# One decoder layer on one core: stick-breaking weights kept as plain products, the last value of each group added at the end, and both instruction plans made anew

## The chip, the cores and the metric

The kernel runs on one core of a Trainium2 chip. The metric is the device time of one execution in microseconds, the median of the runs. Times of single instructions come from one profiled execution.

## The reference, cut to what matters

One layer on x of 1024 tokens by 1024 channels in float32: RMSNorm, one input projection, attention and a convolution module side by side, one output projection with a residual, RMSNorm, a gated up-projection with a short convolution, and a down-projection with a residual. The part that the change touches:

```python
beta[t, s] = sigmoid(q[t] . k[s] / 8)                     # s < t, 8 heads of 64
A[t, s]    = beta[t, s] * prod over s<j<t of (1 - beta[t, j])
o[t]       = sum over s<t of A[t, s] * v[s]
...
x = x + concat([attention, conv]) @ w_out
```

With P[t, s] = the product over s <= j < t of (1 - beta[t, j]), A[t, s] = P[t, s+1] - P[t, s]. So the sum can be written with differences of neighbouring values of v in place of differences of P.

## The kernel before, in words

TensorE takes each float32 product in three passes (high by high, low by high, high by low; `mm3`, L389 to L391), so most operands are made twice: a rounded high copy (mostly on ACT) and a low remainder (VectorE or POOL). Five stages follow each other in the span.

- **Input projections (0 to about 220 us).** Two loads of x per step are squared (L530), scaled (L548), turned (`hT` L556) and split (`h_hi` L560, `h_lo` L561). Weights of v come as `raw_v`, and are scaled into `hi_v` (L593) and `lo_v` (L599); glu weights go through L606 to L622, qk after them. `begin` (L485 to L499) runs idle matmuls while x loads.
- **Attention (about 220 to 411 us).** Heads go one after another, in halves, and queries in groups of 256. For each 128 queries: scores `z` (L1304, L1305) on TensorE, sigmoid(-z) into `nb` on ACT (L1312), a reversed scan of products on VectorE (L1326), `less`, which takes one from the result, on POOL (L1331) or ACT (L1333), transposes `wT` on TensorE (L1353), the high copy (`rest`, or `diagonal` for the block on the diagonal; L1362, L1364), the low (`tl` L1374, `diagonal` L1369), and products `po` with v's differences (L1381). Beyond a query P is one; less one, it is zero there, so keys up to the group's end add nothing. `differences` forms v[s-1] - v[s] once, through `ahead`, which SyncE's DMAs fill with v a row later. Of each `po`, ACT copies one half of the head pair's rows (L1409) and VectorE adds the other half to it (L1412, 64x512) into `attn`. Between these TensorE runs the qk projection and the conv rows of w_out (`op`); the weights of w_out come as `rawo`, with highs `w_hh` and `hio` and lows `w_hl` (L1439) and `loo` (L1531).
- **Handover (about 411 to 492 us).** For each token tile in the order 0, 4, 1, 5, 2, 6, 3, 7: the attention rows of w_out (`opa`; its operand `m` is cast on ACT, L1599 and L1607, with its low on VectorE, L1605 and L1608), the addition to x (L1622), the square on ACT (L1632), the root on POOL, the scaling to `h2` (L1640), the transposes `h2T` (L1648) and the operands `b` and `bT` of a seven-product block scheme (L1660, L1661, sums `raws` and `t`, L1673 to L1698). The first blocks of w_up are `rawu0` and `rawu1`, their operands `a` and `aS` (L385, L386, L1784, L1788). x is stored by tile to `x_d` (L1626).
- **Up-projection (492 to 886 us)** and **down-projection (886 to 1095 us)**, `u`, `u_S` and `dn`.

The work up to the attention's end is one plan and the handover another. Each is a list of operations with a cost and due time; `in_order` issues them on TensorE, VectorE, ACT and POOL in the order of a table of numbers, `ORDERS`, of 1929 and 237 entries, so an instruction runs behind all that stand ahead of it on its engine. An operation that may run on several engines goes by the plan's costs to the one that is free first. SyncE issues the DMAs in one queue, in which one that waits holds those behind it.

## Time and profile before

| | us |
|---|---|
| median of 3 runs | 1103.04 (1102.15 to 1103.22) |
| profiled execution | 1100.73 |
| its span | 1099.0 |
| TensorE busy | 1085.8 |
| VectorE busy | 875.4 |
| ACT busy | 606.6 |
| POOL busy | 609.8 |
| `less` on POOL, 57 instructions | 39.8 |

The profiled execution is 1.7 us longer than its span (work ahead of the first and behind the last recorded instruction). In the profile PE is TensorE, PEld its weight loads, DVE VectorE, POOL GpSimd, and SP SyncE. A row gives the start in us, the duration, the engine, the line, the operation, output <- inputs, shapes and count; a bracket at its end is the engine's idle time just before, with the instruction that ended it.

### The profile page before, as it was taken

Reading aid. Unit: us, or ns where it says so; the run is one execution under the profiler, and the core shown is the slowest. Engines: PE = TensorE matmul, PEld = TensorE weight load, DVE = VectorE, ACT = ScalarE, POOL = GpSimd, SP = SyncE. Lnnn points to the kernel's source line nnn. Section 1 sums busy time; section 2 is a strip of 40 time slices with the busy share of each in tenths; the row PEclk is TensorE's granted clock in tenths of the full one; section 3 lists DMA queues with packets and bytes.
Section 4 is the critical chain, followed back from the end, with each engine's and each line's share of the span. In section 5 each row is a group of like instructions: output and inputs, shape, how many; then the busy total and the mean of one; then the engine's idle time right before and its main releaser. Section 6 shows DMA issues by size and latency. Waiting matters only on the chain.

```text
span 1099.0 us, 14945 instructions
## 1 busy us (share of the span) xinstructions
PE 1085.8 (99%) x5252; PEld 904.1 (82%) x5252; DVE 875.4 (80%) x1178; ACT 606.6 (55%) x1113; POOL 609.8 (55%) x540
## 2 busy tenths in 40 slices
PE   8999999999999999999999999999999999999998
PEld 5888888889888878778888888888888888888887
DVE  6498898689998996899977777677867578697885
ACT  7345467878877665644433333333433388676660
POOL 3377988786654544784333223313322399887760
PEclk9999999999999999999999999999999999999999
DMA  8121210444643324523322312222222572413403
GB/s 272 39 58 52 83 39 19 116 154 143 203 125 97 106 94 161 187 58 116 96 96 67 104 59 96 77 96 77 77 97 67 183 287 78 153 31 124 153 7 147
DMA packets 110249, 117.99 MB, mean 107 GB/s; under 512 B 21114, under 2 KB 89953, under 8 KB 110175
## 3 DMA queue, kind: packets, MB, share of 16 engines
q1 hardware_dynamic: 110158, 117.05, 32.5%
q8 instruction: 41, 0.67, 0.3%
q14 instruction: 34, 0.27, 0.1%
q10 hardware_dynamic: 16, 0.00, 0.0%
HBM read 82.43 MB, written 28.31 MB: 101 GB/s over the span
## 4 chain that ended last, share of the span: by engine, by line
PE 92%; DVE 3%; ACT 1%; DMA 1%; issue 1%; POOL 1%; SPq 0%; DVEq 0%; ACTq 0%
PE dn L1987 19%; PE u_S L391 7%; PE u_S L390 7%; PE u_S L389 7%; PE u L391 5%; PE u L390 5%; PE u L389 5%; PE po L1381 3%; PE qk L389 3%; PE qk L391 3%; PE qk L390 3%; PE wT L1353 2%; PE z L1304 1%; PE glu_b L390 1%; PE op L389 1%; PE glu_b L391 1%
## 5 line engine op out<-in xcount | busy, mean ns | idle before, releaser
L1987 PE MATMUL dn<-wd,wd 128*128 128x512 f32 x768 | 181.4, 389 | 0.0
L1987 PEld LDWEIGHTS dn<-wd,wd 128*128 128x128 f32 x768 | 144.1, 188 | 29.9
L1990 DVE TENSOR_TENSOR c<-dn,c 128x512 f32<-128x512 f32 x120 | 81.4, 685 | 27.6 <-PE dn L1987 27.0
L391 PE MATMUL u_S<-bT,aS 128*128 128x512 f32 x264 | 102.7, 389 | 0.1
L390 PE MATMUL u_S<-bT,aS 128*128 128x512 f32 x264 | 102.5, 389 | 0.0
L389 PE MATMUL u_S<-bT,aS 128*128 128x512 f32 x264 | 102.5, 389 | 0.0
L385 ACT CAST aS<-rawu 128x512 fp32r<-128x512 f32 x63 | 39.0, 621 | 95.2 <-PE u_S L391 68.9
L1892 ACT CAST wd<-rawd 128x512 fp32r<-128x512 f32 x128 | 72.6, 618 | 31.8 <-DMA rawd<-act_d 8.0
L1326 DVE TENSOR_TENSOR_SCAN nb<-nb,one 128x128 f32<-128x128 f32 (+7 forms) x64 | 85.1, 1341 | 1.5 <-ACT nb L1312 1.4
L1733 POOL TENSOR_TENSOR s<-rawu 128x512 f32<-128x512 f32 x21 | 29.6, 1414 | 101.8 <-DMA rawu<-in_w_up_dram 101.8
L1891 ACT COPY whole<-rawd 128x512 f32<-128x512 f32 x110 | 63.4, 585 | 26.0 <-DVE wd L1893 12.9
L1739 POOL TENSOR_TENSOR rawu<-rawu 128x512 f32<-128x512 f32 x21 | 29.5, 1408 | 81.1 <-DVE a L386 81.1
L1893 DVE TENSOR_TENSOR wd<-whole,wd 128x512 fp32r<-128x512 f32 x90 | 59.9, 684 | 12.6 <-ACT wd L1892 6.8
L1331 POOL TENSOR_SCALAR nb<-nb 128x512 f32<-128x512 f32 (+7 forms) x57 | 39.8, 705 | 50.3 <-DVE nb L1326 38.0
L1836 DVE SCALAR_TENSOR_TENSOR y<-gv,cols_a,y 128x1023 f32<-128x1023 f32 (+1 forms) x44 | 59.9, 1361 | 8.9 <-ACT y L1834 8.9
L385 ACT CAST a<-rawu 128x512 fp32r<-128x512 f32 x63 | 38.9, 621 | 48.7 <-PE u_S L391 33.8
L389 PE MATMUL u<-b,a 128*128 128x512 f32 x168 | 65.5, 390 | 0.0
L391 PE MATMUL u<-b,a 128*128 128x512 f32 x168 | 65.4, 389 | 0.0
L390 PE MATMUL u<-b,a 128*128 128x512 f32 x168 | 65.3, 389 | 0.0
L386 DVE TENSOR_TENSOR a<-rawu,a 128x512 fp32r<-128x512 f32 x63 | 50.9, 809 | 13.3 <-ACT a L385 13.3
L1735 POOL TENSOR_TENSOR rawu<-s,rawu 128x512 f32<-128x512 f32 x21 | 32.0, 1527 | 48.6 <-DVE a L386 47.8
L391 PEld LDWEIGHTS u_S<-bT,aS 128*128 128x128 f32 x264 | 49.5, 188 | 10.7 <-DVE aS L386 0.5
(359 smaller groups left out, 3274.5 us busy)
## 6 DMA issues: line engine op xcount, KB each, us to landing
rawu<-in_w_up_dram SPq DMA_DIRECT2D x44, 512.0 KB
act_d<-y SPq DMA_DIRECT2D x22, 512.0 KB
rawd<-act_d SPq DMA_DIRECT2D x22, 512.0 KB
rawd<-in_w_down_dram SPq DMA_DIRECT2D x22, 512.0 KB
raw_qk<-in_w_in_dram SPq DMA_DIRECT2D x16, 256.0 KB
rawo<-in_w_out_dram SPq DMA_DIRECT2D x8, 512.0 KB
m<-conv_d SPq DMA_DIRECT2D x16, 256.0 KB
xt<-in_x_dram SPq DMA_DIRECT2D x8, 512.0 KB
```

The costliest lines, as they stand in the source:

```text
L385: nc.scalar.copy(hi, src)
L386: lo_engine.tensor_tensor(lo, src, f32(hi), op=ALU.subtract)
L389: nc.tensor.matmul(ps, a_hi, b_hi, start=first, stop=False)
L390: nc.tensor.matmul(ps, a_hi, b_lo, start=False, stop=False)
L391: nc.tensor.matmul(ps, a_lo, b_hi, start=False, stop=last)
L1326: nc.vector.tensor_tensor_scan(rev, rev, ones_of[0][:, :w], 0.0, op0=ALU.mult, op1=ALU.max)
L1836: nc.vector.scalar_tensor_tensor(y[:, j:], g[:, :S - j], par("fw", (KF - 1 - j) * NF + f), y[:, j:], op0=ALU.mult, op1=ALU.add)
L1891: nc.scalar.copy(whole, src)
L1892: nc.scalar.copy(t[:, 0], src)
L1893: lo_engine.tensor_tensor(t[:, 1], whole, f32(t[:, 0]), op=ALU.subtract)
L1987: nc.tensor.matmul(ps, a[:, tok], b, start=first and m == 0, stop=last and m == 2, skip_group_check=True)
L1990: nc.vector.tensor_tensor(sums[c][s], ps, sums[c][s], op=ALU.add)
```

## The change

`less` is gone: the transposes take the scanned products as they are. In the half-empty block on the diagonal the upper part is filled with ones in place of zeros. The differences of v over a group then sum with weight one beyond each query to minus the group's last value, so that value is added where the halves are summed: L1412's one instruction of 64x512 becomes two of 64x256 with a column of `v_ends` as a scalar. `differences` gets a step for that: eight DMAs copy the last rows of v, four transposes on TensorE turn them, and two VectorE copies put them into `v_ends`.

```diff
-    minus_one = const([P, 1], F32, "minus_one")
-    nc.vector.memset(minus_one, -1.0)
+    plus_one = const([P, 1], F32, "plus_one")
+    nc.vector.memset(plus_one, 1.0)
...
-        for n in range(7):
+        for n in range(9):
             nc.tensor.matmul(idle, zero_b, zero_b.unsqueeze(1).to_broadcast([P, 4, P]), start=True, stop=True)
...
+        def take_ends():
+            d["ends"] = squares(room, f"ends{blk}")[:4, :256]
+            for n in range(4):
+                nc.sync.dma_start(d["ends"][n:n + 1, :], qkv["v", blk][P - 1:P, 2 * n + 1, :])
+
+        def turn_ends():
+            d["turned"] = bank(s, [P, 2, 4], f"ends{blk}")
+            for c in range(2):
+                nc.tensor.transpose(d["turned"][:, c, :], d["ends"][:, c * P:(c + 1) * P], ident[:4, :4])
+
+        y = add("SP", 2000, take_ends, key, after, [room])
+        m = add("PE", 230, turn_ends, key, [y], [s])
+        kept_ends = add("DVE", 100, lambda: nc.vector.tensor_copy(v_ends[:, 8 * blk:8 * blk + 8].rearrange("p (c t) -> p c t", c=2), d["turned"]), key, [m])
...
-                nc.scalar.copy(diagonal(blk, name)[:, :P], zero_b)
+                nc.scalar.activation(diagonal(blk, name)[:, :P], zero_b, AF.Identity, bias=plus_one if name == "thd" else 0.0)
...
-                def less(eng, d=d, o=o):
-                    nb = d["nb"][:, o:S]
-                    if eng == "POOL":
-                        nc.gpsimd.tensor_scalar(nb, nb, 1.0, -1.0, op0=ALU.mult, op1=ALU.add)
-                    else:
-                        nc.scalar.activation(nb, nb, AF.Identity, bias=minus_one)
-
                 a = add("DVE", 130 + 2.1 * w, scan, i - AHEAD_SCAN + 0.3 * u, ones)
-                b = add({"POOL": 192 + 0.84 * w, "ACT": 296 + 0.84 * w}, less, i - AHEAD_SCAN + 0.3 * u, [a])
-                ws.append((b, d, nbt, o))
+                ws.append((a, d, nbt, o))
...
-                def summed(dst=dst, pd=pd, pa=pa):
-                    nc.vector.tensor_tensor(dst(), pd["po"].rearrange("p a t -> p (a t)")[pa, :], dst(), op=ALU.add)
+                def summed(dst=dst, pd=pd, pa=pa, h=h, half=half):
+                    for a in range(2):
+                        to = dst()[:, a * 256:(a + 1) * 256]
+                        end = 4 * (h // 2) + 2 * half + a
+                        nc.vector.scalar_tensor_tensor(to, pd["po"][pa, a, :], v_ends[pa, end:end + 1], to, op0=ALU.add, op1=ALU.add)
```

Beside that, several operations may now run on another engine (the scaling of x and the high of a weight on ACT or VectorE, `h_hi` on either, lows of w_out on VectorE or POOL, the scaling of q and k also on POOL), costs of the plan are set anew, a DMA's from 3250 to 3500 ns, and both tables of `ORDERS` are replaced whole:

```diff
-1 35 37 14 36 49 2 0 39 41 50 38 40 45 42 3 5 8 51 43 6 16 46 55 11 44 52 119 53 122 56 130 128 15 4 121 28 125 54 25
...
+1720 1869 1870 1724 1725 1726
```

By counts of instructions, VectorE's go from 1180 to 1201, ACT's from 1099 to 1032, POOL's from 545 to 506 and SyncE's from 304 to 312. On VectorE the lows `w_hl` go from 4 to 2 and `loo` from 4 to 1 (the others are on POOL), high copies of `rest` from 2 to 8, the copies of the keys' transposes from 1 to 3, and scalings of x from 16 to 8 (the others are on ACT). SyncE's first `ends` DMA stands just ahead of `raw_glu_b1`, the second ahead of `raw_glu_b2`.

The order of instructions moves at three places (start, end of attention, handover).

TensorE at the start of the program, behind its idle matmuls, before (two tokens' `hT` ahead of `v`; the number after a name tells its tile):

```order
L556 MATMUL hT0_0_223<-ident_r_118,x_k0_138 128x128 x4
L556 MATMUL hT0_1_245<-ident_r_118,x_k0_138 128x128 x4
L556 MATMUL hT1_0_255<-ident_r_118,x_k0_138 128x128 x4
L715 MATMUL v0_260<-hi_v_0_228,h_hi0_175 128x512 x2
L556 MATMUL hT1_1_266<-ident_r_118,x_k0_138 128x128 x4
L715 MATMUL v0_260<-hi_v_1_240,h_lo0_176 128x512
L715 MATMUL v0_260<-hi_v_1_240,h_hi0_175 128x512
```

The same place after:

```order
L555 MATMUL hT0_0_225<-ident_r_118,x_k0_138 128x128 x4
L555 MATMUL hT0_1_236<-ident_r_118,x_k0_138 128x128 x4
L738 MATMUL v0_241<-hi_v_0_231,h_hi0_175 128x512 x2
L555 MATMUL hT1_0_258<-ident_r_118,x_k0_138 128x128 x4
L738 MATMUL v0_241<-hi_v_0_231,h_lo0_176 128x512 x2
L555 MATMUL hT1_1_271<-ident_r_118,x_k0_138 128x128 x4
L738 MATMUL v0_241<-hi_v_1_252,h_hi0_175 128x512 x2
```

The first two `v` products move ahead of the second pair of transposes. On VectorE there, `hi_v` comes in behind the first scaling of x; after:

```order
L548 TENSOR_SCALAR x_k0_138<-x_k0_138,rs0_187 128x512 x2
L597 TENSOR_SCALAR hi_v_0_231<-raw_v_0_220,gain_180 128x512 x2
L561 TENSOR_TENSOR h_lo0_176<-hT0_0_225,h_hi0_175 128x4x128
L597 TENSOR_SCALAR hi_v_1_252<-raw_v_1_246,gain_180 128x512 x2
L561 TENSOR_TENSOR h_lo0_176<-hT0_1_236,h_hi0_175 128x4x128
L561 TENSOR_TENSOR h_lo0_176<-hT1_0_258,h_hi0_175 128x4x128
```

Before, ACT made `hi_v`, and VectorE scaled the second token's x in its place.

VectorE at the end of the attention, from the sum of unit 7_0 (the digits of `wT` and `po` are head, group and key block) on, before:

```order
L1412 TENSOR_TENSOR attn_110<-po7_0_4208,attn_110 64x512
L1531 TENSOR_TENSOR loo2_4296<-rawo_3078,hio2_4295 128x1024
L1326 SCALAR_TENSOR_TENSOR nb0_7_2432<-nb0_7_2432,one_2173 128x1024
L1374 TENSOR_TENSOR tl_2354<-wT7_2_0_4319,rest_2182 128x512
L1364 CAST rest_2182<-wT7_2_1_4331 128x512
L1374 TENSOR_TENSOR tl_2354<-wT7_2_1_4331,rest_2182 128x512
L1369 TENSOR_TENSOR diagonal_1_3285<-wT7_2_2_4337,diagonal_1_3285 128x384
L1374 TENSOR_TENSOR tl_2354<-wT7_3_0_4359,rest_2182 128x512
L1531 TENSOR_TENSOR loo1_4348<-rawo_3078,hio1_4347 128x1024
L1369 TENSOR_TENSOR diagonal_1_3285<-wT7_3_3_4364,diagonal_1_3285 128x384
L1374 TENSOR_TENSOR tl_2354<-wT7_3_1_4382,rest_2182 128x512
```

The same place after:

```order
L1435 SCALAR_TENSOR_TENSOR attn_110<-po7_0_4164,v_ends_103,attn_110 64x256 x2
L1354 SCALAR_TENSOR_TENSOR nb0_2_2246<-nb0_2_2246,one_2085 128x1024
L1394 TENSOR_TENSOR tl_2352<-wT7_2_0_4257,rest_2156 128x512
L1389 TENSOR_TENSOR diagonal_1_3336<-wT7_2_2_4266,diagonal_1_3336 128x384
L1394 TENSOR_TENSOR tl_2352<-wT7_2_1_4273,rest_2156 128x512
L1394 TENSOR_TENSOR tl_2352<-wT7_3_0_4279,rest_2156 128x512
L1384 CAST rest_2156<-wT7_3_1_4299 128x512
L1394 TENSOR_TENSOR tl_2352<-wT7_3_1_4299,rest_2156 128x512
L1389 TENSOR_TENSOR diagonal_1_3336<-wT7_3_3_4305,diagonal_1_3336 128x384
L1394 TENSOR_TENSOR tl_2352<-wT7_3_2_4321,rest_2156 128x512
L1555 TENSOR_TENSOR loo3_4345<-rawo_3323,hio3_4344 128x1024
```

`loo2` and `loo1` are gone from between these rows, and the high copy on VectorE is that of 7_3 in place of 7_2.

ACT in the handover, around the square of token 7 (`h2_7` here), before:

```order
L1784 CAST a22_0_4936<-rawu0_1_4861 128x512
L1673 COPY raws3_4945<-h2T3_0_4931 128x512
L1660 CAST b11_4435<-h2T3_0_4931 128x4x128
L1660 CAST b21_4436<-h2T3_1_4938 128x4x128
L1632 ACTIVATE h2_7_4955,sq2_7_4953<-x2_7_4823 128x1024
L385 CAST a12_1_5124<-rawu1_0_5036 128x512
L385 CAST a11_1_5121<-rawu1_0_5036 128x512
```

And after:

```order
L1686 CAST b11_4368<-h2T3_0_4824 128x4x128
L1716 COPY t2_6_4861<-h2T6_0_4819 128x512
L1686 CAST b21_4369<-h2T3_1_4854 128x4x128
L383 CAST a12_1_5063<-rawu1_0_4975 128x512
L1658 ACTIVATE h2_7_4877,sq2_7_4875<-x2_7_4830 128x1024
L1810 CAST a22_0_4892<-rawu0_1_4849 128x512
L1686 CAST bT1_4372<-raws2_4815 128x4x128
```

The square moved behind the cast of `a12_1`, which reads `rawu1`, and behind token 3's operands. On TensorE half of token 7's `opa` stands between the two transposes of token 3 now, where both transposes followed it before; after (each first of 12 products):

```order
L1674 MATMUL h2T3_0_4824<-ident_r_118,h2_3_4792 128x128 x4
L387 MATMUL opa7_0_4832<-hio0_3788,m7_4707 128x512
L388 MATMUL opa7_0_4832<-loo0_3789,m7_4707 128x512
...
L1674 MATMUL h2T3_1_4854<-ident_r_118,h2_3_4792 128x128 x4
L1674 MATMUL h2T6_1_4869<-ident_r_118,h2_6_4769 128x128 x4
L387 MATMUL u0_11_4879<-b11_4368,a_first_4761 128x512
```

And behind token 7's transposes TensorE reaches the first pass of `u0_S2` after 23 products, where it was 26, and the third, which reads the low of `aS2_0`, after 33, where it was 45; lows of `rawu0` and `rawu1` come in between token 7's operands on VectorE; after:

```order
L1719 TENSOR_TENSOR raws3_4917<-h2T7_0_4923,raws3_4917 128x512
L384 TENSOR_TENSOR a11_1_5060<-rawu1_0_4975,a11_1_5060 128x512
L1720 TENSOR_TENSOR t1_7_4949<-h2T7_1_4943,raws3_4917 128x512
L1687 TENSOR_TENSOR b22_4370<-h2T7_1_4943,b22_4370 128x4x128
L1721 TENSOR_TENSOR t2_7_4950<-h2T7_1_4943,t2_7_4950 128x512
L1687 TENSOR_TENSOR bT1_4372<-raws3_4917,bT1_4372 128x4x128
L1814 TENSOR_TENSOR aS4_0_4958<-rawu0_0_4712,aS4_0_4958 128x512
L1687 TENSOR_TENSOR bT4_4373<-raws3_4917,bT4_4373 128x4x128
L1814 TENSOR_TENSOR aS2_0_4937<-rawu0_0_4712,aS2_0_4937 128x512
```

Before, `a11_1` and `aS2_0` stood ahead of all of token 7's operands there.

More of the change, by code (lines that the diff above doesn't have):

```diff
@@ L559, in norm_in @@
             m = add("PE", 440, turn, T(at_ + 1), [c] + waits, [s])
-            f = add("ACT", 600, lambda i=i, where=where: nc.scalar.copy(h_hi[t // 4][where], d["pt", i]), T(at_ + 1), [m])
+            f = add({"ACT": 600, "DVE": 690}, lambda eng, i=i, where=where: (nc.scalar.copy if eng == "ACT" else nc.vector.tensor_copy)(
+                h_hi[t // 4][where], d["pt", i]), T(at_ + 1), [m])
             e = add("DVE", 690, lambda i=i, where=where: nc.vector.tensor_tensor(
@@ L1129, in square, with scale @@
             nc.scalar.activation(d["squares"], d["ps"], AF.Square)
-        def scale():
+        def scale(eng):
             for n, part in enumerate("qk"):
+                if eng == "ACT":
+                    for i in range(4):
+                        nc.scalar.activation(qkv[part, 1][:, t, i * DH:(i + 1) * DH], d["ps"][:, n * 256 + i * DH:n * 256 + (i + 1) * DH],
+                                             AF.Copy, scale=d["rs"][:, 4 * n + i:4 * n + i + 1])
+                    continue
                 nc.vector.tensor_tensor(qkv[part, 1][:, t, :].rearrange("p (h d) -> p h d", d=DH),
@@ L1140, in queries_keys @@
         c = add("POOL", 1925, lambda: rstd(d["rs"], d["sq"], 1.0 / DH), key(0.5), [b])
-        e = add("DVE", 750, scale, key(0.5), [c])
+        e = add({"DVE": 750, "ACT": 2750}, scale, key(0.5), [c])
         room.users += [b]
@@ L1530, in w_attn_rows @@
         a = add("ACT", 1060, high, key, [x], rooms)
-        b = add("DVE2", 1215, lambda: nc.vector.tensor_tensor(w_attn[k][1], d["raw"], f32(w_attn[k][0]), op=ALU.subtract), key, [a])
+        b = add({"DVE2": 1215, "POOL": 2450}, lambda eng: (nc.vector if eng == "DVE" else nc.gpsimd).tensor_tensor(w_attn[k][1], d["raw"], f32(w_attn[k][0]), op=ALU.subtract), key, [a])
         last_unit.append(b)
```

45 lines of the change are left out of this document (29 added, 16 removed), and 160 rows, old and new, of the table ORDERS.

## The prediction

> **What bounds the kernel now.** I read the page's head, then busy time by stretches of the span (the stretch, its length, then the busy time of TensorE, its weight loads, VectorE, ACT and POOL with their instruction counts, the granted clock, DMA share and GB/s).
>
> ```profile
> span 1099.0 us, 14945 instructions
> PE 1085.8 (99%) x5252; PEld 904.1 (82%) x5252; DVE 875.4 (80%) x1178; ACT 606.6 (55%) x1113; POOL 609.8 (55%) x540
> ...
> PEclk9999999999999999999999999999999999999999
> ```
> ```profile
> 0.00:27.50 27.50, 24.10 (x111) 16.47 (x112) 17.06 (x35) 20.71 (x38) 8.90 (x24) 1.00 0.81 272
> 27.50:220.00 192.50, 192.50 (x886) 159.33 (x886) 149.99 (x219) 108.84 (x226) 145.71 (x127) 1.00 0.20 58
> ...
> 275.00:302.50 27.50, 26.41 (x174) 23.29 (x173) 26.40 (x30) 24.43 (x57) 18.79 (x19) 1.00 0.66 200
> ...
> 385.00:412.50 27.50, 25.27 (x167) 21.78 (x165) 26.12 (x33) 18.79 (x35) 11.08 (x12) 1.00 0.29 96
> ...
> 440.00:467.50 27.50, 25.81 (x127) 20.73 (x126) 23.74 (x34) 19.08 (x37) 21.10 (x25) 1.00 0.55 181
> 467.50:495.00 27.50, 26.65 (x120) 21.39 (x120) 27.28 (x29) 12.40 (x22) 24.32 (x15) 1.00 0.20 58
> 495.00:1072.50 577.50, 577.50 (x2550) 478.18 (x2549) 447.46 (x599) 284.78 (x462) 279.51 (x207) 1.00 0.30 102
> 1072.50:1100.00 27.50, 22.79 (x101) 18.54 (x99) 14.67 (x23) 1.14 (x2) 1.29 (x1) 0.99 0.38 143
> ```
>
> TensorE bounds it: 1085.8 of 1099.0 us at full granted clock. So `less`, which ran on POOL and ACT, is no saving by itself; only TensorE's idle time can shrink. Subtract busy from length in each row: 3.40 us are missing at the start, none to 220, 1.09 in the middle of the attention, 2.23 at its end, 1.69 and 0.85 in the handover to the up-projection, none to 1072.5, and the last row holds the tail (4.71, of which 1.0 lies beyond the span). The products of the up- and down-projection keep their order, so nothing is to be won or lost from 495 on. The four places ahead of it hold 9.3 us; VectorE is busy 26 to 27 of 27.5 us in three of those rows, and is what TensorE waits for there. TensorE's rows at these places:
>
> ```profile
> 8.96 0.66 PE L556 MATMUL hT<-ident_r,x_k 128*128 128x128 f32 x4 [0.69 <-DVE x_k L548]
> 9.84 0.73 PE L715 MATMUL v<-hi_v,h_hi 128*128 128x512 f32 x2 [0.22 <-ACT h_hi L560]
> ...
> 281.37 0.53 PE L1226 MATMUL kT<-ident_r,keys 128*128 128x128 f32 x4 [0.61 <-DVE rest L1267]
> ...
> 400.38 0.60 PE L1353 MATMUL wT<-ident_r,nb 128*128 128x128 f32 x4
> 400.74 0.48 PE L389 MATMUL op<-w_hh,m 128*128 128x512 f32 x1
> ...
> 403.50 0.64 PE L1353 MATMUL wT<-ident_r,nb 128*128 128x128 f32 x4
> 404.45 0.52 PE L1353 MATMUL wT<-ident_r,nb 128*128 128x128 f32 x3 [0.32 <-DVE tl L1374]
> ...
> 407.83 0.39 PE L1381 MATMUL po<-tl,rest 128*128 128x256 f32 x1 [0.41 <-DVE tl L1374]
> ...
> 411.05 0.50 PE L389 MATMUL opa<-hio,m 128*128 128x512 f32 x1 [1.40 <-ACT m L1607]
> ...
> 463.40 0.50 PE L389 MATMUL u<-b,a_first 128*128 128x512 f32 x1 [0.81 <-ACT b L1660]
> 464.49 0.47 PE L390 MATMUL u<-b,a_first 128*128 128x512 f32 x1 [0.59 <-DVE b L1661]
> ...
> 470.68 1.29 PE L1648 MATMUL h2T<-ident_r,h 128*128 128x128 f32 x8 [0.71 <-ACT gv L1825]
> ```
>
> Each bracket is the idle time ahead of a row and what ended it. Matmuls overlap, so true loss is a little more: the four transposes at 403.50 take 0.95 us to the next row, those at 400.38 only 0.36.
>
> **The change, part by part.** First the swap on VectorE and POOL:
>
> ```profile
> L1331 POOL TENSOR_SCALAR nb<-nb 128x512 f32<-128x512 f32 (+7 forms) x57 | 39.8, 705 | 50.3 <-DVE nb L1326 38.0
> ...
> 245.60 0.41 DVE L1133 TENSOR_TENSOR qk<-qk,rs_qk 128x256 f32<-128x256 f32 x1
> ...
> 398.13 0.69 DVE L1412 TENSOR_TENSOR attn<-po,attn 64x512 f32<-64x512 f32 x1
> 398.86 1.23 DVE L1531 TENSOR_TENSOR loo<-rawo,hio 128x1024 fp32r<-128x1024 f32 x1
> 400.11 2.29 DVE L1326 TENSOR_TENSOR_SCAN nb<-nb,one 128x1024 f32<-128x1024 f32 x1
> ```
>
> POOL loses 39.8 us. VectorE pays: each 64x512 addition becomes two 64x256 ones with a scalar operand. The trace has no such instruction. Its bounds are half of 0.69 (0.34) and the 256-wide row out of PSUM (0.41); I take 0.40, the nearer in shape. So 32 x 0.40 - 16 x 0.69 = 12.8 - 11.0 = **+1.8 us of VectorE** over 180, 0.1 a pair.
>
> *The last values.* Four small transposes are new on TensorE, at most 0.36 us together by the four at 400.38, with nothing to hide them: **+0.25**. Their eight row copies stand in SyncE's queue, the first ahead of the second glu weights, and wait for v's copies out of PSUM; TensorE was not idle once from 27.5 to 220, so I cost the queue at 0, and at +1.5 us if a weight came late. Two more idle matmuls sit where TensorE waits for x anyway: 0.
>
> *The start.*
>
> ```profile
> 6.63 0.88 DVE L548 TENSOR_SCALAR x_k<-x_k,rs 128x512 f32<-128x512 f32 x2 [0.90 <-POOL rs L534]
> ...
> 7.98 1.34 ACT L593 ACTIVATE hi_v<-raw_v,gain 128x512 fp32r<-128x512 f32 x2 [0.56 <-DMA raw_v<-in_w_in_dram]
> 9.22 0.56 ACT L560 CAST h_hi<-hT 128x512 fp32r<-128x512 f32 x1
> ```
>
> The first `v` product now waits for `h_hi` behind `hi_v` on ACT (7.98 + 1.34 = 9.3, then the cast). After, VectorE makes `hi_v` when the load lands: 7.98 + 0.88, the time of an equal pair in row 6.63, is 8.9; ACT casts `h_hi` at once. So `v` can start at 8.9 instead of 9.84, and the second token's transposes, now after the first two products, find their x scaled on ACT. All 0.91 us of the two idle brackets could go; `h_lo` now queues behind `hi_v` on VectorE, which may return some. Between -0.9 and +0.3, taken **-0.6**.
>
> *The middle of the attention.*
>
> ```profile
> 277.46 3.19 DVE w_hl L1439 x2
> ```
>
> In the chain, two lows of w_out, 3.19 us, run on VectorE just before the `rest` for which TensorE's keys wait 0.61. Two of four such lows go to POOL, as do three of four `loo` (1.23 each): 5 x 1.22 = 6.1 us off VectorE, and `less` drops out between scan and transposes. But the new plan gives VectorE six more casts, two more key casts and part of the scaling: by counts and these durations its sum over the attention is about even (near 183 us either way). The place moves, the load does not: between -1.1 (all idle gone) and +1, taken **-0.4**.
>
> What do the lows cost on POOL? Two-input work of POOL beside VectorE:
>
> ```profile
> 291.03 4.19 DVE L1326 TENSOR_TENSOR_SCAN nb<-nb,one 128x1024 f32<-128x1024 f32 x2
> ...
> 293.09 1.30 POOL L1487 TENSOR_TENSOR xt<-prod,xt 128x512 f32<-128x512 f32 x1 [0.84 <-ACT prod L1484]
> ...
> 277.14 1.28 POOL L1212 TENSOR_TENSOR rest<-v,rest 128x512 fp32r<-128x512 f32 x1
> ```
>
> The two scans took 4.19 us with POOL's 1.30 inside; one of 1024 alone takes 2.29, so they were not held. The two `w_hl` took 3.19 instead of 2 x 1.22, with POOL's 1.28 inside. Scans are what VectorE mostly runs here, so I price POOL's lows at nothing, and `less`'s end at nothing for the scans too. [...]
>
> *The end of the attention.* Around the last scan VectorE runs `loo` at 398.86 and again two ahead of the last units' lows; both go to POOL, and the last scan is followed by transposes without `less` (0.70 us on average). TensorE loses 0.41 at 407.83, 0.95 - 0.36 = 0.59 at 403.50, and some small gaps: about 1.5 in all. I leave 0.6 of it for the cast of `rest` that stays on VectorE: **-0.9**, between -1.5 and 0. The 1.40 ahead of `opa` stays: copy, addition (+0.1) and cast still follow the last product.
>
> *The handover.*
>
> ```profile
> 457.01 5.05 DMA x_d<-x
> ...
> 462.14 4.06 DMA rawu<-in_w_up_dram
> ...
> 462.47 0.68 DVE L1622 TENSOR_TENSOR x<-opa,x 128x512 f32<-128x512 f32 x1
> ...
> 464.26 1.06 ACT L1632 ACTIVATE h<-x 128x1024 f32<-128x1024 f32 x1
> ```
>
> The first `u` waits of 0.81 and 0.59 stand right behind token 3's transposes; half of `opa7` is now put between these, 12 products of 0.23 us (577.50 us over 2550 in the row from 495), so both go: -1.4. Against it, token 7's square on ACT now stands behind the cast of `a12_1`, whose load follows token 3's store: 5.05 + 4.06 and a cast (0.56 by the one at 9.22), 9.7 us after token 3's addition. By the order, TensorE runs 24 products and four transposes of four, 24 x 0.23 + 4 x 0.36 = 7.0 us, from token 3's last product to token 7's, so the square is held 2.7 us behind its input, against 464.26 - 463.15 = 1.1 before (463.15 is the end of the row at 462.47): +1.6 on transposes that already waited 0.71. Lows of the first blocks also come later on VectorE: bounded by 0 and three such rows of 0.68, 2.0; I take 0.6, as most find cover. Together **+0.8**, between -2.1 (all three waits go and nothing is late) and +4.6 (1.6 and 2.0 in full, 1.0 at token 7's own operands, and nothing gained).
>
> **Sum:** +0.25 - 0.6 - 0.4 - 0.9 + 0.8 = **-0.85 us**. The profiled execution took 1100.73 us, so 1099.9; the runs shown have a median of 1103.04, 2.3 us above, so I forecast **1102.2 us**.
>
> **The rivals.** *Faster:* VectorE's queue loosens where TensorE waits, and the handover is repaired as well. -0.9 - 1.1 - 1.5 - 2.1 + 0.25 = -5.4 gives 1097.7; four fifths of it 1098.7. For it: all but one of the idle rows carry a VectorE releaser or an ACT one fed by it. Against: its load is even. *Slower:* the held square of token 7. ACT is in order, so behind `a12_1` wait the square, `a22_0` and every later high; the pass of `u0_S2` that reads `aS2_0`'s low now comes 33 products behind token 7's transposes, 33 x 0.23 = 7.6 us, where there were 45. From the point at which that low, now behind all of token 7's operands on VectorE, ends more than 7.6 us after those transposes, each microsecond is one of TensorE. At +4.6 here, with the rest at half its gain (-0.8), it is 1106.8; at +3.5 it is 1105.7. For it: VectorE is 27.28 of 27.5 us busy there. Against: the store of token 3 may be quicker under another queue order. *Scans held by POOL:* a low of 1024 on POOL is some 2.6 us (twice the 1.30 at 293.09); if each of the five held a scan, and two of them where TensorE waits for VectorE, 5.2 us come on top: 1107.4. Against it stand the scans at 291.03; I give it 0.03. [...] *The change doesn't do what it says:* new waits in the attention eat the gain, since VectorE's sum is even, and it stays within 1 us of 1103.04.
>
> **How the numbers follow.** About 0.2%, 2.2 us, is what a measurement can tell from no change. Forecast with the case of no effect 0.42 (both within 2.2 us); faster rival 0.36; slower 0.22, of which 0.03 for the held scans. The range takes four fifths of the faster case's gain and the slower one's lesser price: 1098.6 to 1105.9; the likeliest alone would be 1101 to 1104.
>
> **What would show it.** Right: no `L1331` rows and no POOL time between scan and transposes; `v` starting near 8.9; no `loo` on VectorE between 397 and 405; the pair near 0.8 us; no wait at the first `u`; a wait of 1 to 2 us at token 7's transposes, released through its square. Wrong: pairs of over 1 us, a wait in 27.5 to 220 (a weight load behind the row copies), TensorE idle over 3 us in 440 to 495, or any in 495 to 1072, where I count on nothing.

## The result and the profile after

The changed kernel takes **1108.7 us** (median of four runs, 1108.42 to 1108.98), beside 1103.03 for the kernel before: a ratio of 1.0056, 95% interval 1.0044 to 1.0068 (the plain quotient of the two medians is 1.0051). It is slower by 5.7 us, where the prediction said 1102.2 and at most 1105.9. The profiled execution took 1108.43 us.

The head of the page of the changed kernel:

```profile
span 1106.6 us, 14845 instructions
...
PE 1088.9 (98%) x5258; PEld 906.7 (82%) x5258; DVE 879.2 (79%) x1199; ACT 587.6 (53%) x1046; POOL 591.1 (53%) x501
...
PEclk9999999999999999989999999999999999999999
```

POOL and ACT each lost 19 us, VectorE gained 4, and TensorE, with six more matmuls, is busy 3.1 us longer: its clock row has an 8. Busy time by stretches, with the columns of the prediction's table:

```profile
0.00:27.50 27.50, 23.30 (x105) 15.68 (x106) 18.34 (x33) 20.56 (x37) 13.11 (x26) 1.00 0.81 272
27.50:220.00 192.50, 192.50 (x885) 158.97 (x885) 157.62 (x222) 102.26 (x197) 139.43 (x124) 1.00 0.19 55
220.00:275.00 55.00, 54.46 (x344) 46.84 (x342) 50.03 (x72) 39.26 (x78) 40.81 (x42) 1.00 0.44 140
275.00:302.50 27.50, 27.42 (x183) 24.57 (x181) 25.60 (x35) 20.94 (x40) 19.82 (x15) 1.00 0.89 258
...
385.00:412.50 27.50, 26.35 (x172) 23.11 (x170) 24.61 (x32) 17.50 (x32) 9.84 (x6) 1.00 0.25 90
412.50:440.00 27.50, 26.57 (x126) 21.91 (x127) 14.96 (x24) 11.24 (x26) 9.09 (x16) 1.00 0.43 152
440.00:467.50 27.50, 27.50 (x141) 23.09 (x140) 21.33 (x33) 16.95 (x34) 22.06 (x23) 1.00 0.59 199
467.50:495.00 27.50, 20.26 (x84) 15.78 (x83) 23.89 (x26) 15.49 (x29) 21.73 (x17) 0.88 0.20 58
495.00:1072.50 577.50, 577.50 (x2550) 478.34 (x2549) 447.03 (x600) 287.65 (x466) 286.03 (x210) 1.00 0.30 102
```

Subtract busy from length again. The start misses 4.20 us (3.40 before), the middle of the attention 0.08 (1.09), its end 1.15 (2.23) with 0.93 (0) in the next row, into which most of the wait of 1.40 us ahead of the first `opa` product has moved. The row from 440 misses nothing (1.69), and that from 467.5 **7.24** (0.85), at a clock of 0.88. From 495 on nothing changed. One row holds the loss. In it, TensorE's timeline, from the last product of `opa` on:

```profile
462.62 0.39 PE L389 MATMUL opa<-hio,m 128*128 128x512 f32 x1
462.86 1.03 PE L1674 MATMUL h2T<-ident_r,h 128*128 128x128 f32 x8
463.64 0.48 PE L387 MATMUL u<-b,a_first 128*128 128x512 f32 x1
...
468.96 0.39 PE L389 MATMUL u<-b,a_first 128*128 128x512 f32 x1
470.80 0.63 PE L1674 MATMUL h2T<-ident_r,h 128*128 128x128 f32 x4 [1.46 <-DVE h L1666]
472.46 0.63 PE L1674 MATMUL h2T<-ident_r,h 128*128 128x128 f32 x4 [1.03 <-ACT aS L1810]
477.45 0.79 PE L387 MATMUL u<-b,a 128*128 128x512 f32 x1 [4.36 <-ACT a L383]
478.04 0.63 PE L388 MATMUL u<-b,a 128*128 128x512 f32 x1
478.47 0.63 PE L387 MATMUL u<-b,a 128*128 128x512 f32 x1
...
481.03 0.44 PE L387 MATMUL u<-b,a 128*128 128x512 f32 x1
481.30 0.39 PE L388 MATMUL u<-b,a 128*128 128x512 f32 x1
...
496.94 0.39 PE L387 MATMUL u<-bT,a 128*128 128x512 f32 x1
```

After the last `opa` product come 24 products on `a_first`, token 7's transposes after 1.46 and 1.03 us of waiting, and then 4.36 us in front of `u1_11`, the first product of the second block. Behind that wait products start 0.43 us apart instead of 0.23 for 3.6 us (478.04, 478.47 and so on to 481.03), so some 1.8 us go without any idle time. The granted clock, in steps of 0.05 us, stands at half from 474.3 to 481.1 us, so it fell within the wait. The row at 496.94 is the hundredth `u` or `u_S` product behind the last `opa` product: the **handover's length**, from the one start to the other, is 34.3 us here and 27.5 in the kernel before (461.33 to 488.83). With it the two profiled executions add up: the last `opa` product starts 1.3 us later, the handover is 6.8 longer, the rest 0.4 shorter, and the last matmul ends 7.7 later (1102.98 against 1095.29). That is 2.0 more than between the medians, because the profiled execution of before was 2.3 below its median. It ran at a granted clock of 1.000 throughout, where most executions of that kernel have a mean of 0.997 or 0.998 (those at 0.998 have a median of 1102.6 us, those at 1.000 of 1101.3); and the three profiles of kernels with the same start (before_pairs, old_new_handover, before_t6_late) show 0.66 to 0.69 between 10 and 15 us. So the start from which the prediction reads its gain was probably better than usual. All later kernels are measured with this length too.

What ACT does meanwhile:

```profile
467.24 0.62 ACT L383 CAST a<-rawu 128x512 fp32r<-128x512 f32 x1 [3.17 <-DMA rawu<-in_w_up_dram]
467.77 1.06 ACT L1658 ACTIVATE h<-x 128x1024 f32<-128x1024 f32 x1
...
473.93 0.59 ACT L1686 CAST b<-h2T 128x512 fp32r<-128x512 f32 x1
474.40 0.59 ACT L1851 COPY gv<-u 128x512 f32<-128x512 f32 x1
...
476.78 0.62 ACT L383 CAST a<-rawu 128x512 fp32r<-128x512 f32 x1 [0.81 <-DVE bT L1687]
```

It stands still for 3.17 us until `rawu1` has landed (the prediction's rival had this: the square of token 7 behind `a12_1`). Then it runs without a gap to 475.9: casts for tokens 6 and 7 and the first blocks, 0.52 us each. Among them is `gv`, the copy of `u0_11` out of PSUM, which frees the bank that `u1_11` needs. VectorE has as much to do: 24 instructions from token 7's last addition to the low of `aS2_0`, both counted, where there were about 13. And lows took longer beside POOL's work. Two of them, the first with POOL idle (0.69 us), the second beside two lows on POOL (1.75):

```profile
467.89 0.69 DVE L384 TENSOR_TENSOR a<-rawu,a 128x512 fp32r<-128x512 f32 x1 [2.36 <-ACT a L383]
...
473.27 1.75 DVE L1814 TENSOR_TENSOR aS<-s,aS 128x512 fp32r<-128x512 f32 x1
```

### The profile page after: what moved, and what is told of

The parts are those of the page before. It is cut to its first block, busy times and chain, and to the rows that moved or that the text cites. A ratio compares the mean times of both kernels' runs of the same rounds, so it can differ in the third digit from the quotient of the medians.

```text
span 1106.6 us, 14845 instructions
## 1 busy us (share of the span) xinstructions
PE 1088.9 (98%) x5258; PEld 906.7 (82%) x5258; DVE 879.2 (79%) x1199; ACT 587.6 (53%) x1046; POOL 591.1 (53%) x501
## 4 chain that ended last, share of the span: by engine, by line
PE 94%; DVE 3%; DMA 1%; issue 0%; ACT 0%; POOL 0%; SPq 0%; DVEq 0%; POOLq 0%
PE dn L2013 19%; PE u_S L389 7%; PE u_S L388 7%; PE u_S L387 7%; PE u L388 5%; PE u L389 5%; PE u L387 5%; PE po L1401 3%; PE wT L1373 3%; PE qk L387 3%; PE qk L389 3%; PE qk L388 3%; PE z L1332 2%; PE z L1333 1%; PE glu_b L389 1%; PE glu_b L387 1%
## 5 line engine op out<-in xcount | busy, mean ns | idle before, releaser
L1759 POOL TENSOR_TENSOR s<-rawu 128x512 f32<-128x512 f32 x21 | 29.5, 1406 | 106.8 <-DMA rawu<-in_w_up_dram 94.7
L1354 DVE TENSOR_TENSOR_SCAN nb<-nb,one 128x384 f32<-128x384 f32 (+7 forms) x64 | 85.0, 1341 | 1.2 <-ACT nb L1340 0.9
L384 DVE TENSOR_TENSOR a<-rawu,a 128x512 fp32r<-128x512 f32 x63 | 47.1, 748 | 14.5 <-ACT a L383 14.5
L389 PEld LDWEIGHTS u_S<-bT,aS 128*128 128x128 f32 x264 | 49.6, 188 | 11.0 <-DVE aS L1814 0.8
L387 PEld LDWEIGHTS u_S<-bT,aS 128*128 128x128 f32 x264 | 49.6, 188 | 10.3
L388 PEld LDWEIGHTS u_S<-bT,aS 128*128 128x128 f32 x264 | 49.6, 188 | 10.3
```

The lines of the kernel that those rows point to most:

```text
L384: lo_engine.tensor_tensor(lo, src, f32(hi), op=ALU.subtract)
L387: nc.tensor.matmul(ps, a_hi, b_hi, start=first, stop=False)
L388: nc.tensor.matmul(ps, a_hi, b_lo, start=False, stop=False)
L389: nc.tensor.matmul(ps, a_lo, b_hi, start=False, stop=last)
L1354: nc.vector.tensor_tensor_scan(rev, rev, ones_of[0][:, :w], 0.0, op0=ALU.mult, op1=ALU.max)
```

## The experiments

The time is the median; the ratio is to runs of the kernel before on the same chip, and differs from the plain quotient of the two medians by up to 0.0006 (for act_order_lows 1103.33 over 1102.75 is 1.0005); the length is the handover's in the profiled execution, which differed by 1.3 us between two profiles of the changed kernel.

| kernel | us | ratio (95%) | length |
|---|---|---|---|
| before | 1103.03 | 1 | 27.5 |
| changed | 1108.7 | 1.0056 (1.0044 to 1.0068) | 34.3 |
| new_old_handover | 1104.62 | 1.0020 (1.0011 to 1.0030) | 27.3 |
| old_new_handover | 1107.05 | 1.0045 (1.0029 to 1.0062) | 33.6 |
| algebra_only | 1106.95 | 1.0035 (1.0022 to 1.0048) | 27.5 |
| algebra_single | 1103.79 | 1.0014 (1.0005 to 1.0024) | 27.4 |
| before_pairs | 1102.82 | 1.0009 (0.9998 to 1.0019) | 27.3 |
| v_low_dve | 1107.70 | 1.0050 (1.0035 to 1.0065) | 33.8 |
| old_handover_v_low | 1104.42 | 1.0027 (1.0013 to 1.0040) | 28.4 |
| square_first | 1107.82 | 1.0053 (1.0038 to 1.0068) | 32.6 |
| own_sq | 1107.94 | 1.0047 (1.0032 to 1.0062) | 32.4 |
| lows_off | 1108.78 | 1.0052 (1.0037 to 1.0067) | 33.1 |
| lows_zero | 1108.59 | 1.0052 (1.0037 to 1.0067) | 34.0 |
| t6_first | 1110.06 | 1.0066 (1.0049 to 1.0083) | 35.1 |
| before_t6_late | 1111.18 | 1.0082 (1.0065 to 1.0099) | 35.7 |
| fillers | 1106.43 | 1.0038 (1.0025 to 1.0052) | 32.4 |
| both_limits | 1108.34 | 1.0051 (1.0037 to 1.0065) | 31.4 |
| act_order | 1104.58 | 1.0014 (1.0005 to 1.0024) | 29.5 |
| act_order_lows | 1103.33 | 1.0000 (0.9991 to 1.0010) | 27.3 |
| after_again | 1108.80 | 1.0051 (1.0031 to 1.0071) | 33.1 |

### Which part of the change costs: the tables swapped

The second table of `ORDERS`, the handover's, fits both kernels. One kernel is the changed one with the table of before, the other the kernel before with the new table:

```diff
-0 4 26 6 7 5 28 29 10 3 27 1 11 8
...
+0 4 26 5 6 3 27 7 28 25 56 8 29 1
...
```

> The changed kernel with the table of the handover's plan (the second of ORDERS) taken from before. Theory H (the handover's new order costs the time): from the first opa product to the last u_S the changed kernel lost 5.4 us more than before, and these come back, 1108.7 - 5.4 = 1103.3 us, with no wait over 1.5 us behind token 7's transposes. Rival A (the attention with its new algebra and plan brings the handover its late start or a full VectorE): it stays above 1107.

> The kernel before with only the handover's table from the change. Theory H: 1103.0 + 5.4 = 1108.4 us, with a wait of about 4 us ahead of u1_11. Rival A: under 1104.5.

With the old table the changed kernel is 0.20% above before instead of 0.56%; the new table alone makes the old kernel 0.45% slower, with the same wait in the same place (waits for TensorE of old_new_handover: engine and line that waited, what for, sum, times, longest):

```profile
PE u L389 <- ACT a L385: 4.4, 1, 4.4
```

So the handover's table costs 4 to 5 us of the 5.7 (0.36 and 0.45% of 1103), and by these two runs the rest of the change costs 1 to 2, where the prediction had a gain. The last experiment below, act_order_lows, keeps that rest, has a handover as short as new_old_handover's, and comes out level with the kernel before; so the rest is bounded only between nothing and about 2 us.

### The rest: algebra without new tables, the pair, the start

The new arithmetic in the kernel before, each operation at its old place (`less` gone, the steps for `v_ends` put in):

```diff
-                b = add({"POOL": 192 + 0.84 * w, "ACT": 296 + 0.84 * w}, less, i - AHEAD_SCAN + 0.3 * u, [a])
-                ws.append((b, d, nbt, o))
+                ws.append((a, d, nbt, o))
...
-                    nc.vector.tensor_tensor(dst(), pd["po"].rearrange("p a t -> p (a t)")[pa, :], dst(), op=ALU.add)
+                    for a in range(2):
...
+                        nc.vector.scalar_tensor_tensor(to, pd["po"][pa, a, :], v_ends[pa, end:end + 1], to, op0=ALU.add, op1=ALU.add)
```

> The kernel before with the algebra alone: no less, ones above the diagonal, last values added in the two halves, and both tables of before with the 64 less taken out and the six new steps put in; costs and engines' choices as before. Theory G (scanned products used at once free VectorE and POOL in the attention, and the loss came with the tables alone): 1101.5 to 1103, nothing lost in the handover. Rival E (the pairs of additions, the last values' copies and transposes cost more than less did): 1104 or more.

The same with before's single addition, so the last value of each group is missing from the attention (algebra_single), and the kernel before with the pair, its scalar a constant zero (before_pairs):

```diff
-                    nc.vector.tensor_tensor(dst(), pd["po"].rearrange("p a t -> p (a t)")[pa, :], dst(), op=ALU.add)
+                    for a in range(2):
+                        to = dst()[:, a * 256:(a + 1) * 256]
+                        nc.vector.scalar_tensor_tensor(to, pd["po"][pa, a, :], 0.0, to, op0=ALU.add, op1=ALU.add)
```

> The kernel algebra_only with the sums made by one instruction of 64x512 again: each group's last value is then missing from the attention's result; its copies and transposes still run. Theory P: without the pairs the algebra is worth what less took from the chain between scan and transposes, 1101 to 1103. Rival S (a scan's end now comes straight before the transposes, and what TensorE waits for is VectorE's order of scans and lows, or the slow clock): 1105 or more, as algebra_only.

> The kernel before with the sums of the halves made by two instructions of 64x256 with a constant scalar, as the change does, in place of one of 64x512; less stays. Theory P (the pair of 0.96 us for 0.69 on a full VectorE is what the algebra costs): 1104 to 1106 against 1102.5. Rival: VectorE has room for 16 x 0.27 = 4.3 us, 1102 to 1103.

By itself the algebra brings no gain: 0.14 to 0.35% slower in the old order, by intervals that stay above one. The pair costs at most 0.19% where only it changes. In algebra_only's profile the handover is as long as before, and the loss lies ahead of it: at the attention's end waits of 0.84, 0.45 and 0.34 us stand in front of `po` and `op`, and at the first `opa` products, from 417.45 to 420.84, products start 0.43 us apart, some 1.6 us. That fall of the clock isn't the algebra's alone: old_new_handover and before_t6_late, with before's attention, show a granted clock of 0.94 between 412.5 and 440 too, and before and before_pairs 1.00. How much of the loss is the algebra's stays open. The group of the pair's instructions in the changed kernel (count, then ns of the shortest, the median and the longest):

```profile
L1435 DVE SCALAR_TENSOR_TENSOR attn<-po,v_ends,attn x24: 452/480/494, 247.0 to 413.0; 64x256 f32<-64x256 f32 x24
```

The start of the changed kernel, in its timeline:

```profile
8.82 0.88 DVE L597 TENSOR_SCALAR hi_v<-raw_v,gain 128x512 fp32r<-128x512 f32 x2 [1.55 <-DMA raw_v<-in_w_in_dram]
...
9.41 1.53 POOL L605 TENSOR_SCALAR raw_v<-raw_v,gain 128x512 f32<-128x512 f32 x2
...
9.46 0.81 PE L738 MATMUL v<-hi_v,h_hi 128*128 128x512 f32 x2 [1.24 <-DVE hi_v L597]
...
10.29 3.43 DVE L597 TENSOR_SCALAR hi_v<-raw_v,gain 128x512 fp32r<-128x512 f32 x2
...
11.03 2.41 POOL L607 TENSOR_TENSOR lo_v<-raw_v,hi_v 128x1024 fp32r<-128x1024 f32 x1
...
13.77 0.97 PE L738 MATMUL v<-hi_v,h_hi 128*128 128x512 f32 x3 [1.86 <-DVE hi_v L597]
```

`v` does start at 9.46 instead of 9.84, but the second pair of `hi_v` takes 3.43 us where the first takes 0.88, beside POOL's two instructions, and TensorE waits 1.86 for it. An experiment put the lows of v on VectorE alone, in the changed kernel and in the one with the old handover:

```diff
-            b = add({"DVE2": 1480, "POOL": 3700}, low, T(at_ - LEAD_W + 0.5), [a])
+            b = add({"DVE2": 1480} if name[0] == "v" else {"DVE2": 1480, "POOL": 3700}, low, T(at_ - LEAD_W + 0.5), [a])
```

> The changed kernel with the lows of v's weights kept on VectorE, so that POOL does not work on raw_v beside VectorE's hi_v at the start. Theory P (POOL's work stretched the second hi_v pair from 0.9 to 3.43 us): that pair takes about 0.9, the wait of 1.86 at the third v product goes, 1.5 to 1.9 us gained, 1107.0. Rival L (the pair waits for its load): no gain, 1108.4 to 1109.

> The changed kernel with before's table for the handover and the lows of v's weights on VectorE: both repairs together. If they add up, 1.5 us under new_old_handover's 2.3 us above before: 1103.3 against 1102.5; a start that hangs on when the loads land: 1104.5 to 1105.

In v_low_dve the second pair takes 0.88 us and the wait of 1.86 is gone, so POOL's work was what stretched it. TensorE's idle time in the first 27.5 us fell from 4.2 to 2.6 us, but neither time fell by more than its uncertainty; in old_handover_v_low a wait of 2.3 us for `h_lo` stands behind 27.5 us in its place. Between profiles the start differs by more: in kernels that share the changed start the first `v` product begins between 8.42 us (lows_zero) and 10.57 (square_first), in those that share before's between 9.84 (before) and 11.03 (before_pairs). So what the new start costs or brings is left open.

### Why the handover waits: first guesses, all too small

Square of token 7 ahead of the cast of `a12_1` (square_first); that and a buffer of its own for `a11_1` (own_sq, which also holds back the cast of `a11_1`, and whose second edit is the last pair of lines):

```diff
+            if f == 1 and name == "12":
...
+                tc.add_manual_dep(cast, squared[7].name, mybir.DependencyInfo(
+                    mybir.DependencyClass.NoSync, mybir.DependencyReason.DATA), reason="behind the square")
...
-            if name in ("11", "22"):
+            if name in ("11", "22") and not (f == 1 and name == "11"):
```

> The changed kernel with one instruction moved: the high cast of a12_1 on ACT is held behind token 7's square, both orders tables as changed. Theory S (ACT stands 3.2 us at that cast for the load of rawu1, and all behind it is late): the square runs 3.3 us earlier, the waits of 1.5 and 1.0 at token 7's transposes go, the one of 4.4 ahead of u1_11 shrinks to 2 or less and the clock does not fall: 1103.5 to 1105. Rival D (VectorE's queue of first operands and blocks is what u1_11 waits for): at most 1.5 us gained, 1107 or more.

> The changed kernel with a11_1 in a buffer of its own (it had to wait for token 6's sums to be read by VectorE) and with the casts of rawu1 behind token 7's square on ACT. Theory B (the held buffer is the cost): u1_11 follows token 7's transposes at once, 4.4 us and the slow clock behind it go, 1103. Theory D: the wait of 4.4 us goes, but token 7's operands still stand behind the same work on VectorE, so that TensorE waits 4 us or more at its first u_S instead; 1.5 us gained at most, 1107.2 or more.

With the square first the waits at token 7's transposes are gone and `u1_11` waits 5.9 us instead of 4.4: the time stays. With the buffer as well, the waits of own_sq behind the last `opa` product are these:

```profile
PE u L387 <- ACT gv L1858: 2.2, 1, 2.2
PE u L387 <- DVE gv L1859: 1.4, 1, 1.4
PE u_S L387 <- ACT bT L1687: 1.1, 1, 1.1
PE u_S L389 <- DVE aS L1821: 0.5, 1, 0.5
```

Again 5.2 us in all, now for other things. The next theory was the amount of work on VectorE. Three lows were written as zeros: in lows_off `bT3` and `bT4` of token 6 and `aS1` of the first block, by ACT in their place; in lows_zero `bT3`, `bT4` and `b22` of token 6, by ACT some 25 us earlier. This leaves these parts of the products out. In t6_first only the order changed, operands of the first blocks behind those of token 6. The edit of lows_zero:

```diff
-            e = add(lows, lambda eng: (nc.vector if eng == "DVE" else nc.gpsimd).tensor_tensor(
+            e = add({"DVE": 1}, lambda eng: None, key, [a]) if t == 6 and name in ("T3", "T4", "22") else \
...
+            for name in ("T3", "T4", "22") if t == 4 else ():
+                nc.scalar.activation(B[name][1][:, :, 2 * P:3 * P], d["b", 0], AF.Copy, scale=0.0)
```

> The changed kernel with three lows of the handover (bT3 and bT4 of token 6, aS1 of the first block) left out: they are written as zeros by ACT instead of computed on VectorE, so three small remainders are missing from the up-projection's operands. Nothing else moves. Theory D (VectorE's queue between 464 and 487 us sets both the start of u1_11 and that of u_S): these three took 1.1 + 1.75 + 1.75 us there, so u1_11 starts 3.5 to 4.5 us earlier, its wait is under 1 us and the clock stays; 1108.7 - 4.5 = 1104.2, range 1103.5 to 1105.2. Rival L (the load of rawu1 and ACT, or TensorE's own order, set it): at most 1 us gained, 1107.7 or more.

> The changed kernel with three low ends of token 6's operands (bT3, bT4 and b22 of its blocks) left out: they are written as zeros by ScalarE some 25 us earlier, so neither VectorE nor ScalarE has them in the stretch from 463 to 485 us, and the products are less exact. Theory D (VectorE's pile of operand work behind the last first-block product sets the first sum product): the first rank-one update of token 7's second block starts 2 to 4 us earlier, its wait of 4.36 us shrinks below 2, the clock stays up, and the kernel gains 3 to 5 us against the changed kernel beside it, to about 1104 to 1105.5. Rival (ScalarE's queue with the cast behind the late weight transfer sets it): the wait stays above 3 us and the gain is 1 us or less.

> The changed kernel with the operands of the first-block products of the sum moved behind token 6's operands in the handover's order; the amount of work is the same. Theory D (the amount of work behind 463 us against 5.5 us of cover): the wait ahead of the rank-one update shrinks, but the first sum products wait for about as much; at most the clock's 1.8 us come back, about 1106.5. Rival (the place of those first operands ahead of token 6's is the cause): both waits shrink and 4 us come back, about 1104.

> The changed kernel as it is, beside the two others on the same chip: 1108 to 1108.7 us, 5.7 us above the kernel before.

The theory missed. With three lows gone VectorE stands idle, and `u1_11` still waits 3.0 us (5.0 in lows_off, where ACT has them on top), for ACT, whose row in lows_zero runs unbroken from 467.2, after 3.25 us of standing still, to the cast of `a11_1`. The clock is low for longer there: it stands at half from 472.3 to 482.5, 10.2 us instead of 6.8, which takes back part of what the shorter wait gave. In t6_first ACT works through token 6 first and `u1_11` waits 6.6.

The other way round: in the kernel before, token 6's transposes and operands behind token 3's transposes, where the new table has them.

```diff
-143 128 145 216 130 188 144 146 147 170 189 151 217 171 148
+143 128 145 216 130 188 170 189 217 171 172 218 173 191 190 219 174 176 175 221 177 144 146 147 151 148
...
```

> The kernel before with one thing of the new handover: token 6's transposes and the sums and operands made from them stand behind token 3's transposes, as in the change, where they stood 24 opa products earlier. Theory T (the new order spends TensorE's opa products first and leaves the operands of tokens 6 and 7 the 24 u products behind it as only cover): TensorE waits 3 us or more between token 7's transposes and the first u_S, the clock falls once more: 1105 to 1108 against 1102.5. Rival O (the first blocks' operands ahead of token 7's on VectorE and the cast ahead of the square on ACT are the cause): under 1103.5.

```profile
473.04 0.80 PE L382 MATMUL u<-b,a_first 128*128 128x512 f32 x1 [6.49 <-ACT b L1653]
```

This alone costs 0.82% in the old order, with a low clock behind the wait. But the wait is at another place than in the changed kernel, and than theory T had it: the sixteen transposes of tokens 3 and 6 stand directly behind the last `opa` product, and the first product on `a_first` waits 6.49 us for its operand `b` on ACT; behind token 7's transposes TensorE has no wait over 0.2 us. So moving token 6's operand work behind the products that covered it is dear by itself, but this run doesn't show that it is what `u1_11` waits for.

The clock's share: ten idle products into `u1_11`'s own bank, ahead of its first real one, to keep TensorE working in the wait.

```diff
+        if f == 1 and a == "11":
+            for _ in range(10):
+                nc.tensor.matmul(ps.rearrange("p (a b) -> p a b", a=4), zero_b, zero_b.unsqueeze(1).to_broadcast([P, 4, P]), start=True, stop=True)
```

> The changed kernel with ten idle bf16 matmuls of 128x512 put ahead of u1_11 into its own bank, where TensorE waits 4.4 us. Theory K (the clock that falls to half behind this wait costs 9 x 0.2 = 1.8 us by itself): the products from u1_11 on run at 0.23 us from the first, 1.5 to 1.8 us gained, 1107. Theory D: they run at full clock but the pass of u_S that waits for VectorE at 487.3 waits so much longer, no gain: 1108.2 to 1109.

The idle products begin at 476.15, once the bank is free, and the real ones run at 0.23 us from 480.23 on:

```profile
476.15 4.00 PE L1779 MATMUL u<-zero_b 128*128 128x512 bf16 x10 [1.95 <-ACT gv L1854]
479.81 0.58 PE L387 MATMUL u<-b,a 128*128 128x512 f32 x1
480.23 0.39 PE L388 MATMUL u<-b,a 128*128 128x512 f32 x1
```

The handover is 1.9 us shorter than in the first profile of the changed kernel (0.7 than in after_again), and the ratio 0.18% smaller, by intervals that overlap: about what the slow stretch costs by its spacing, 1.8 of the 5.7 us, but not clear of the noise. The idle products did not keep the clock up: it stands at half from 476.25 to 479.7, under them, and is back for the real ones. The run also tells that the bank comes free late, through `gv`.

### What settles it: ACT's row mended

Both edits at once, own_sq and lows_zero:

> The changed kernel with both earlier edits at once: the two casts of the second block's operands behind token 7's square, in a buffer of their own, and three low ends of token 6 (bT3, bT4, b22) left out (zeros, written 25 us earlier). Each alone brought 0 to 1 us. Theory E (two queues of about equal length end just ahead of the first rank-one products, ScalarE's, which stands 3.2 us still for the weight transfer, and VectorE's, which holds token 6's low ends; either alone still sets the time): together they bring 3 to 5 us against the changed kernel (1108.7, or 5.7 over before), to about 1104 to 1105.5; the waits ahead of the rank-one update and the first sum product sum to under 3 us, and the clock stays up behind them. Rival (something else sets it, neither queue, or the clock falls whatever the waits are): the sum of the waits stays above 4 us and the gain below 1.5 us.

Still no gain, and the one wait left is for ACT's copy `gv`:

```profile
PE u L387 <- ACT gv L1861: 4.4, 1, 4.4
```

`gv` is not in the plan; in the changed kernel it stands, from the square on, behind thirteen other instructions of ACT. Last, ACT's row was mended: `gv` becomes a step of the plan, into a buffer that is free (`gv_3`), behind the first six of these, and the two casts that wait for `rawu1` stand behind token 6's `bT3`. Nothing is left out in act_order; act_order_lows has lows_zero's edit too.

```diff
+        def first_out():
+            gv.append(mixp.tile([P, S], F32, tag="attn_2", name="gv_3"))
+            nc.scalar.copy(gv[0][:, :HS], begun["11"])
+
+        add("ACT", 600, first_out, BEGIN_AT, [begun["op", "11"]])
...
+                tc.add_manual_dep(cast, stood[6, "T3"].name, mybir.DependencyInfo(
+                    mybir.DependencyClass.NoSync, mybir.DependencyReason.DATA), reason="behind the cast")
...
-179 154 158 197
+179 237 154 158 197
```

> The changed kernel, nothing left out, with ScalarE's order at the handover mended: the copy of the first product's result, behind which the next block's first product waits for its bank, stands six casts earlier, and the two casts that wait for the late weight transfer stand behind token 6's bT3 instead of ahead of the square, in a buffer of their own. Theory F (ScalarE's order, with its 2.5 to 3.2 us of standing still for the transfer, is what the first product waits for; VectorE's low ends are next): the first product of the second block starts about 10 us after the last first-block product of the operator instead of 14.5; VectorE's low ends then bound the sum product, so the gain against 1108.7 is 1 to 3 us. Rival (VectorE's pile alone sets it): the first product still waits over 4 us and the gain is under 1 us.

> The same mend with the three low ends of token 6 (bT3, bT4, b22) left out as before. Theory F: both queues are short now, the waits from the last product of the operator to the first sum product add up to under 3 us, the clock stays up, and the gain is 3 to 5 us, to about 1104 to 1105.5. Rival (a third limit, or the start and the attention's new order keep the time up whatever the handover does): the waits shrink and the time does not follow, or the waits stay above 4 us.

TensorE's and ACT's rows of act_order:

```profile
463.73 0.39 PE L382 MATMUL opa<-hio,m 128*128 128x512 f32 x1
...
470.30 1.03 PE L1667 MATMUL h2T<-ident_r,h 128*128 128x128 f32 x8
471.37 0.50 PE L380 MATMUL u<-b,a 128*128 128x512 f32 x1
...
474.94 0.59 PE L382 MATMUL u<-b,a 128*128 128x512 f32 x1 [1.97 <-DVE a L377]
475.33 0.63 PE L380 MATMUL u<-b,a 128*128 128x512 f32 x1
```
```profile
466.14 0.61 ACT L1813 CAST a<-rawu 128x512 fp32r<-128x512 f32 x1
466.65 0.62 ACT L1680 CAST bT<-raws 128x512 fp32r<-128x512 f32 x1
467.17 1.07 ACT L1696 COPY raws<-h2T 128x512 f32<-128x512 f32 x2
468.12 0.60 ACT L1844 COPY gv<-u 128x512 f32<-128x512 f32 x1
...
470.68 1.16 ACT L376 CAST a<-rawu 128x512 fp32r<-128x512 f32 x2
```

ACT no longer stands still, token 7's transposes wait for nothing, and `u1_11` starts 7.6 us behind the last `opa` product instead of 14.8. What is left is the low of `a` on VectorE, 1.97 us, and 3.4 us of low clock behind it. The kernel takes 1104.58 us, 0.14% above before (0.05 to 0.24%): about 4 of the 5.7 us are back. With the three lows out of VectorE's queue a wait as long as act_order's is left, but the clock stays up behind it, the handover is as long as before, and the ratio is 1.0000 (0.9991 to 1.0010):

```profile
475.54 0.50 PE L382 MATMUL u<-b,a 128*128 128x512 f32 x1 [2.18 <-DVE a L377]
475.88 0.40 PE L380 MATMUL u<-b,a 128*128 128x512 f32 x1
```

Theory F's mechanism held, and its rival, VectorE alone, fell; the gains were larger than it said (4.1 us where it had 1 to 3, then 1103.33 where it had 1104 to 1105.5). The copy and the two casts were moved in one edit, so the share of each isn't shown. No kernel tried is faster than the one before.

## Why the prediction was wrong, point by point

- **Sign and size.** Forecast 0.85 us faster, measured 5.7 slower. Of the terms of its sum the handover failed most: +0.8, between -2.1 and +4.6, against +6.8 in the profiled execution, about 1.8 of it the clock, which the sum did not have.
- **The step that failed** is the price of the new order at the handover. The waits of 0.81 and 0.59 at the first `u` did go (the row 440 to 467.5 is full), and the square of token 7 was held behind `a12_1`, with 2.5 us of waits at its transposes, against 2.3 worked out; that they agree is partly luck, for 1.03 of them were for another cast of ACT. But the prediction stopped there. It took what else is late for three rows of 0.68, 2.0 us, "as most find cover". The cover was gone: the table spends its `opa` products early, and brings token 6's operands behind the last of them, where 24 products of 0.23 us are all that TensorE has. It looked for the next wait at the low of `aS2_0`, 33 products later; it was at `u1_11`, for a copy and a cast on ACT that the plan's table doesn't hold: own_sq and both_limits wait for the copy, and act_order, which moves both, brings about 4 us back. The rows of 0.68 were mis-sized too: beside POOL such lows took 1.75 to 1.78 us.
- **The held square as the cause** (the slower rival, 1105.7 to 1106.8) was the right place and the wrong mechanism: square_first took those waits away and got nothing back.
- **The start:** -0.6, measured +0.8 by the windows of one pair of profiles, which is within what the start differs by between profiles. `v` was to start at 8.9 and started at 9.46, and a pair of `hi_v` priced at 0.88 took 3.43 beside POOL. The term's upper end, +0.3, came from `h_lo` alone.
- **The attention:** the middle lost 1.0 us less, better than -0.4, but 0.35 came back from 220 to 275. The end was to bring -0.9 and brought -0.15 (2.23 before, 1.15 + 0.93 after). With the start the last `opa` product stands 1.3 us later, where the sum had it 1.65 earlier. The pair, priced at 0.40 us an instruction, took 0.48, so 4.3 us more on VectorE instead of 1.8 (32 x 0.48 - 16 x 0.69). VectorE's sum from 220 to 412.5 came out even as counted (177.2 us before, 176.6 after).
- **Right:** nothing from 27.5 to 220 (+0.25 for four transposes, a queue at no cost) and nothing from 495 on; no scan was held by POOL (the longest took 2.29 us before and after, so the rival's 5.2 us shows in neither profile); `less` was no saving by itself, as algebra_only shows without any new table. The range's ends stand 0.1 and 0.2 us outside the two prices that they are taken from (1098.7 and 1105.7), which changes nothing here.

## What to carry to other kernels

When a table moves work behind a stage's last long run of products, count what each engine must still do until the next run starts, against the cover left, and include the instructions that the table does not hold. Look first for the copy that frees the bank and for casts that wait on a load: ACT ran its list in order here, and the cast that waited 3.17 us for `rawu1` held all behind it. If one repair only moves the wait to another name, look for what else stands in the same queue, and for a second queue that ends nearly as late: here a copy on ACT set the time until it was moved, and VectorE's lows set the rest.
